# A two-layer hybrid decoder on one core: block sums of the feed-forward activations formed in its first part, three feature pairs summed in PSUM in the second, mLSTM scores on full rows

## The chip, the cores and the metric

The kernel runs on 1 core of one Trainium2 chip, as one program. The metric is the time of one execution on the device, in microseconds, as the median of several runs. Its engines are TensorE (PE: matmuls; PEld: weight loads beside them), VectorE (DVE), ScalarE (ACT), GpSimd (POOL) and SyncE (SP), whose queue issues the DMA transfers.

## The reference

Two layers, sequence 1024, width 1024, all in float32. A layer has four token mixers side by side, an output projection, a LayerNorm, a gated feed-forward block and a second LayerNorm. The change touches the mLSTM mixer and the feed-forward block:

```python
def _mlstm_chunkwise(q, k, v, i_pre, f_pre):          # chunks of 128, 4 heads of 64
    ...
        d_log = b_cum[:, :, :, None] - b_cum[:, :, None, :] + ic[:, :, None, :]
        d_log = jnp.where(causal, d_log, -jnp.inf)
        ...
        w_intra = jnp.exp(d_log - m_t[..., None])
        sqk = jnp.einsum('bthd,bshd->bhts', qc, kc) * w_intra
        ...
h = (jax.nn.silu(x @ w_gate[l]) * (x @ w_up[l])) @ w_down[l]     # 1024 -> 2816 -> 1024
x = _layer_norm(DEEPNORM_ALPHA * x + h, ln2_g[l], ln2_b[l])
```

## The kernel before

**Precision.** The large products are float32 to some 22 bits: each operand is split into a high half in the matmul type fp32r (ScalarE casts) and a low half (the difference, on VectorE or GpSimd), and three matmuls of 128x512 make one product: high-high, high-low, low-high. Each tile of 1024 columns holds both halves of 512.

**Order of the work.** The Tile framework places the instructions: within each engine they stand in an order that it chooses by program order and by a simulated timeline, with waits for data and for free buffers. Only in the mLSTM (`mix_d`) is PE's order that of the program. SP issues DMAs in its queue's order.

**mLSTM (`mix_d`).** Eight chunks of 128 tokens. Per chunk, `stage_s` forms a row of weights (`pw`: a matmul that selects one row of `NC`, 40 rows high), four exponentials on ScalarE, a causal mask on GpSimd, and the scores `psc`: for each of 4 heads a float32 matmul of 64 rows by 128 columns (TensorE runs it as two passes), the heads of odd number on rows 64 to 127, each followed by two of the next chunk's projection matmuls (`zvo`, `self.fill(2)`). VectorE multiplies scores and weights in two operations. `stage_n` and `stage_u` make the output and the state update (`pi`, `pn`, `pk`, `pu`, updates of `ds`); `stage_y` transposes the output (`ptd`). All of these have full 128 rows. `stage_s(c + 1)` runs ahead of `stage_n(c)`.

**First part of the feed-forward (`ffn1`, `evac1`).** The hidden features are taken as 11 pairs of 128-feature tiles, the tokens as two halves of 512. Each 2x2 block product is made with 7 products (Strassen's scheme in Winograd's form, numbers 1 to 7 in the order `ORDER = (1, 6, 2, 7, 5, 3, 4)`) instead of 8. A gate tile m and the up tile m + 1 follow each other; `evac1` adds the products up on VectorE into `Ra`, `Rb` (pool R, 8 buffers), applies SiLU to the gate and multiplies. The four blocks of a pair go to `hs` in DRAM as two tiles of 512 KB. The weights `fw` come through 4 buffers, are combined and split into `fc` (6 buffers), four products ahead.

**Second part (`ffn2`).** The same 7-product scheme over 9 pairs; the last two pairs (`std`) go by plain products (`dl`). For each pair `load` brings two tiles of h (`hr`) and two of w (`dr`), `combos` forms the sums of their blocks (four VectorE operations for h, four for w) and splits them: the high half on ScalarE, the low half on GpSimd, for w of the pairs 1, 3 and 5 on VectorE. The pairs are taken in groups: pair 0 alone, then two and two. A step is one group and one product number. In a step each of the four row blocks j opens one PSUM bank, sums 3 matmuls per pair of the group there (`dn`), and closes it; then VectorE adds the bank to an accumulator in SBUF (`ma`, `mb`, `mc`, `md`; in the first group ScalarE copies into ma and mb). mc and md start as x1, the input of the block. In the last group `finish` joins the accumulators, one to three VectorE operations per step and j. `comb` prepares operands up to `AHEAD = 2` steps before their use, in 14 tiles (`operand`). Eight PSUM banks rotate. Behind the groups, `hsplit` and two loops split h and w of the last two pairs, and `dl` products, the second LayerNorm and, in layer 1, the transposes (`ptx`) for the next layer follow.

Of the kernel before, what the change touches and what calls it, by code (L numbers as in the profile page):

```python
# [7 lines left out]
F32 = mybir.dt.float32  # L8
# [5 lines left out]
L = 2  # L14
# [43 lines left out]
class Net:  # L58
# [85 lines left out]
    def consts(self):  # L144
# [5 lines left out]
        sel = cp.tile([40, 8], F32, name="self32")  # L150
        nc.sync.dma_start(sel, io["c_sel"])
        self.sel = cp.tile([40, 8], F32R, name="sel")
# [229 lines left out]
    def mix_d(self, l, T):  # L382
# [6 lines left out]
        def gates():  # L389
# [75 lines left out]
            NC = dr[0:40, 0:512]  # L465
            nc.vector.tensor_scalar(out=NC, in0=self.ident[0:40, 0:1].to_broadcast([40, 512]), scalar1=0.0, scalar2=None, op0=ALU.mult)
# [117 lines left out]

        def stage_s(c):
            tok = tok_of(c)
            pw = self.psum("pw", "mm")
            nc.tensor.matmul(pw, lhsT=self.sel[:, c:c + 1].to_broadcast([40, 128]), rhs=NC, start=True, stop=True)
# [11 lines left out]
            for e_ in range(2):  # L600
                w2 = w4[:, e_:4:2, :]
                nc.vector.tensor_tensor(out=w2, in0=psc[e_][:, 0:256].rearrange("p (h t) -> p h t", h=2), in1=w2, op=ALU.mult)
# [74 lines left out]
        nc.vector.memset(Cf, 0.0)  # L677
        stage_s(0)
# [682 lines left out]
    def evac1(self, l, m, i, pz, R):  # L1361
# [44 lines left out]
        if up and i == (5 if early else 3):  # L1406
            nc.sync.dma_start(io["hs"][l, 2 * f], ra)
        if up and i == 4:
            nc.sync.dma_start(io["hs"][l, 2 * f + 1], rb)
            R.pop(m - 1), R.pop(m)  # L1410

    def ffn2(self, l, last):
# [4 lines left out]
        self.open(x=4, b=4, a=4, c=4, d=4, p=6, o=4)  # L1417
        raws, cmb = {}, {}

        def load(q):  # L1420
            hr = [self.u("hr", F32, "A") for _ in range(2)]
            wr = [self.u("dr", F32, "A") for _ in range(2)]
            for i in range(2):
                nc.sync.dma_start(wr[i], io["wD"][l, 2 * q + i])
                nc.sync.dma_start(hr[i], io["hs"][l, 2 * q + i])
            raws[q] = (hr, wr)
# [6 lines left out]
        groups = [[0]] + [[q, q + 1] for q in range(1, NP - 2, 2)]  # L1433
        std = [NP - 2, NP - 1]

        steps = [(g, i) for g in range(len(groups)) for i in ((1, 6, 7, 5) if g == 0 else ORDER)]
# [4 lines left out]
        def operand(s):  # L1441
            nonlocal nx
            nx += 1
            return self.u(s, F32R, "ooooppppppxxxx"[(nx - 1) % 14])

        def comb(g, i):
            for q in (groups[0] if g == 1 and i in early else []) + groups[g]:
                if q not in cmb:
                    if q not in raws:
                        load(q)  # L1450
                    (h0, h1), (w0, w1) = raws[q]
                    s2 = [self.t2("s2") if g == 0 else None for _ in range(2)]
                    cmb[q] = (self.combos("S", h0[:, lo_], h1[:, lo_], h0[:, hi_], h1[:, hi_], self.t2("s1"), nc.gpsimd, v, s2[0]),
                              self.combos("T", w0[:, lo_], w0[:, hi_], w1[:, lo_], w1[:, hi_], self.t2("s1"), v if q in (1, 3, 5) else nc.gpsimd, v, s2[1]))
                ts = []
                for x in range(2):
                    t = operand("dc")
                    cmb[q][x][i](t)
                    ts.append(t)
                Wc.setdefault((g, i), []).append(ts)  # L1460
# [224 lines left out]
```

## Time and profile before

| | us |
|---|---|
| median of 3 runs (2536.72 to 2543.18) | 2540.49 |
| the profiled execution | 2537.39 |
| its span, first to last instruction | 2535.7 |
| PE busy in it | 2405.2 (95%) |
| DVE busy | 1674.2 (66%) |
| POOL busy | 1347.0 (53%) |
| ACT busy | 1038.7 (41%) |

A line of the timeline gives the start, the time from the first start to the last end of the merged instructions, the engine, the line of the kernel, the operation with output and inputs, their number, and in brackets how long the engine had been idle and who released it. Matmuls overlap: one of 128x512 shows as some 0.39 us, but the next starts 0.23 us after it, so their pitch is read from starts. The clock column is the granted TensorE clock, 1.00 for 2.4 GHz and 0.50 for 1.2 GHz; a mean between stands for a stretch that had both.

### The profile page before, as it was taken

To read this page: it belongs to the slowest core of one execution; us is meant where nothing else is said; L and a number is where in the kernel's file an instruction comes from. 1 tells how busy PE (TensorE), PEld (TensorE's weight loads), DVE (VectorE), ACT (ScalarE), POOL (GpSimd) and SP (SyncE) were. 2 spreads that over 40 slices of the span, in tenths; PEclk is the share of its full clock that TensorE was granted. 3 is DMA by queue.
4 is the path that set the end of the run, shared out by engine and by line. 5 is a ranking of instruction groups with operands and counts; after the bars stand their busy time and mean duration, and the time that the engine had idled before them with its cause. 6 is when DMAs were issued, how large, how long until landed. Compare 5 with 4: busy or idle time off the path is not lost. (4 is left out here: it accounts for less than half of the span.)

```text
span 2535.7 us, 33381 instructions
## 1 busy us (share of the span) xinstructions
PE 2405.2 (95%) x11884; PEld 1993.6 (79%) x11884; DVE 1674.2 (66%) x3040; ACT 1038.7 (41%) x2102; POOL 1347.0 (53%) x1148
## 2 busy tenths in 40 slices
PE   9999878998999999999899999889989999999997
PEld 9779867786888888777697798777868888887775
DVE  7643587478545555999956435874785455559998
ACT  6323568534332333434243235685343323334431
POOL 2013546667554444889520145366665454557894
PEclk9999999999999999999999999899999999999998
DMA  4101101421222224512221110014212222245221
GB/s 162 51 27 41 29 9 56 158 100 54 79 83 95 72 84 150 199 74 76 79 89 43 33 40 23 9 56 158 100 66 69 88 94 67 84 157 192 75 75 67
DMA packets 62807, 206.95 MB, mean 82 GB/s; under 512 B 8546, under 2 KB 10914, under 8 KB 62642
## 3 DMA queue, kind: packets, MB, share of 16 engines
q1 hardware_dynamic: 62642, 204.82, 23.3%
q8 instruction: 95, 1.56, 0.2%
q14 instruction: 70, 0.57, 0.1%
HBM read 158.62 MB, written 46.17 MB: 81 GB/s over the span
## 5 line engine op out<-in xcount | busy, mean ns | idle before, releaser
L119 PE MATMUL gu<-T,fc 128*128 128x512 f32 x2640 | 636.1, 397 | 18.7 <-POOL T L1323 6.1
L119 PEld LDWEIGHTS gu<-T,fc 128*128 128x128 f32 x2640 | 499.6, 190 | 141.6 <-POOL T L1323 8.4
L1248 POOL TENSOR_TENSOR fc<-fw,fc 128x512 fp32r<-128x512 f32 x264 | 366.9, 1393 | 366.5 <-ACT fc L1247 362.5
L119 PE MATMUL dn<-dc,dc 128*128 128x512 f32 x1512 | 361.6, 399 | 20.0 <-DVE md L1512 5.4
L119 PEld LDWEIGHTS dn<-dc,dc 128*128 128x128 f32 x1512 | 285.3, 190 | 96.0 <-DVE ma L1512 7.8
L1247 ACT CAST fc<-fw 128x512 fp32r<-128x512 f32 x264 | 162.7, 620 | 379.3 <-PE gu L119 212.0
L1372 DVE TENSOR_TENSOR Ra<-Ra,gu 128x512 f32<-128x512 f32 x172 | 117.4, 684 | 228.8 <-PE gu L119 225.7
L119 PE MATMUL gu<-B,fc 128*128 128x512 f32 x1056 | 260.5, 395 | 0.0
L119 PEld LDWEIGHTS gu<-B,fc 128*128 128x128 f32 x1056 | 197.8, 188 | 46.9
L1248 POOL TENSOR_TENSOR dc<-hr,dc 128x512 fp32r<-128x512 f32 x104 | 167.8, 1622 | 46.4 <-ACT dc L1247 45.6
L805 POOL TENSOR_SCALAR P<-P,rs 128x256 f32<-128x256 f32 (+7 forms) x128 | 99.5, 782 | 126.7 <-DVE rs L804 108.4
L119 PE MATMUL po<-wh,yT 128*128 128x512 f32 x512 | 162.2, 396 | 0.0
L132 POOL TENSOR_TENSOR wl<-raw,wh 128x768 fp32r<-128x768 f32 (+2 forms) x40 | 81.9, 2054 | 114.8 <-ACT wh L127 114.6
L119 PE MATMUL zc<-wh,xT 128*128 128x384 f32 x512 | 134.1, 339 | 0.0
L1247 ACT CAST dc<-hr 128x512 fp32r<-128x512 f32 x104 | 64.6, 621 | 150.7 <-PE dn L119 47.0
L119 PE MATMUL sc<-kst,q 128*128 128x512 f32 (+3 forms) x384 | 110.9, 384 | 13.6 <-DVE mn L798 13.5
L822 PE MATMUL pt<-ident,P 128*128 128x128 f32 x576 | 92.1, 283 | 23.3 <-DVE PL L141 14.4
L119 PEld LDWEIGHTS po<-wh,yT 128*128 128x128 f32 x512 | 95.7, 188 | 21.8
L802 ACT ACTIVATE P<-P,mn 128x256 f32<-128x256 f32 (+7 forms) x128 | 99.5, 779 | 27.0 <-DVE mn L798 25.4
L1248 POOL TENSOR_TENSOR dc<-dr,dc 128x512 fp32r<-128x512 f32 x68 | 109.1, 1605 | 0.0
L119 PE MATMUL dl<-wl,hl 128*128 128x512 f32 x384 | 97.5, 412 | 11.7 <-DVE mc L1512 9.6
L141 DVE TENSOR_TENSOR PL<-pt,PH 128x512 fp32r<-128x512 f32 (+3 forms) x176 | 95.0, 558 | 20.5 <-ACT PH L138 19.4
(380 smaller groups left out, 5123.9 us busy)
## 6 DMA issues: line engine op xcount, KB each, us to landing
fw<-in_wGU SPq DMA_DIRECT2D x88, 512.0 KB, 3.7
dr<-in_wD SPq DMA_DIRECT2D x44, 512.0 KB, 5.8
hr<-hs SPq DMA_DIRECT2D x44, 512.0 KB, 6.2
hs<-Ra SPq DMA_DIRECT2D x22, 512.0 KB, 2.6
hs<-Rb SPq DMA_DIRECT2D x22, 512.0 KB, 2.9
raw<-in_wO SPq DMA_DIRECT2D x16, 512.0 KB, 3.6
x<-x SPq DMA_DIRECT2D x16, 512.0 KB, 2.6
raw<-in_wC SPq DMA_DIRECT2D x16, 384.0 KB, 3.0
```

The costliest lines, as they stand in the source:

```text
L119: self.nc.tensor.matmul(out, lhsT=a, rhs=b, start=first and j == 0, stop=last and j == n - 1)
L132: (eng or nc.gpsimd).tensor_sub(lo[:, :n], raw[:, :n], f32(hi[:, :n]))
L141: (lo_eng or nc.vector).tensor_sub(lo, src, f32(hi))
L802: nc.scalar.activation(P[:, 0:nk], P[:, 0:nk], AF.Exp, scale=-1.0, bias=m, accum_out=rs[:, 0:1])
L805: nc.gpsimd.tensor_scalar(out=P[:, 0:nk], in0=P[:, 0:nk], scalar1=rs[:, 1:2], scalar2=1.0, op0=ALU.mult, op1=ALU.mult)
L822: nc.tensor.transpose(pt[:, b * 128:(b + 1) * 128], P[:, (b0 + b) * 128:(b0 + b + 1) * 128], self.ident)
L1247: nc.scalar.copy(dst[:, 0:512], src)
L1248: lo_eng.tensor_sub(dst[:, 512:1024], src, f32(dst[:, 0:512]))
L1372: tt = lambda o, a, b, op: v.tensor_tensor(out=o, in0=a, in1=b, op=op)
```

## The change

Three things.

1. mLSTM: the selecting matmul `pw` reads 128 rows of `NC` (the others are zero). The queries of a chunk are copied by GpSimd (`spread`, four copies of 64x128) into a zeroed tile `qz`, two heads side by side as diagonal blocks, two chunks ahead. The scores are then two matmuls of 128 rows by 256 columns into one bank, each followed by four `zvo` matmuls, and one VectorE multiplication.
2. ffn1: for the 9 pairs that take the 7-product scheme in ffn2, `evac1` forms the block sums of h (four more VectorE operations, in the gate's freed tiles) and stores all in `hs` as four parts, 1.75 MB a pair instead of 1 MB.
3. ffn2: three groups of three pairs. `comb` loads each half tile of h (256 KB, pool h of 6 half tiles) that a step needs, split by ScalarE and GpSimd; only w is combined, its low halves on GpSimd for one pair of three and on VectorE for two. A step opens four banks and takes one pair after the other, 12 matmuls each; the banks close at the end. 15 operand tiles; `AHEAD = 1`. w of the next group is loaded in the third step of a group, x1 at the first and fourth step.

```diff
+    def uh(self, s, dt=F32, p="h"):
+        return self.pools[p].tile([128, 512], dt, name=self.nm(s), tag="h" + p)
...
-            NC = dr[0:40, 0:512]
+            NC = dr[:, 0:512]
...
+        qz = self.u("qz", F32, "E")
+        nc.gpsimd.memset(qz, 0.0)
+        QZ = [[qz[:, (2 * b + p) * 256:(2 * b + p + 1) * 256] for p in range(2)] for b in range(2)]
...
-            nc.tensor.matmul(pw, lhsT=self.sel[:, c:c + 1].to_broadcast([40, 128]), rhs=NC, start=True, stop=True)
+            nc.tensor.matmul(pw, lhsT=self.sel[:, c:c + 1].to_broadcast([128, 128]), rhs=NC, start=True, stop=True)
...
-            psc = [self.psum("psc", "s") for _ in range(2)]
-            for hh in range(4):
-                rows = slice(64 * (hh % 2), 64 * (hh % 2) + 64)
-                nc.tensor.matmul(psc[hh % 2][:, hh // 2 * 128:(hh // 2 + 1) * 128], lhsT=QK[2 + hh // 2][rows, tok], rhs=QK[hh // 2][rows, tok], start=True, stop=True)
-                self.fill(2)
...
+            psc = self.psum("psc", "s")
+            for pr_ in range(2):
+                nc.tensor.matmul(psc[:, pr_ * 256:(pr_ + 1) * 256], lhsT=QK[2 + pr_][:, tok], rhs=QZ[c % 2][pr_], start=True, stop=True)
+                self.fill(4)
+            nc.vector.tensor_tensor(out=w, in0=psc, in1=w, op=ALU.mult)
+            spread(c + 2)
...
+        def spread(c):
+            if c < NT:
+                for p in range(2):
+                    for e in range(2):
+                        rows = slice(64 * e, 64 * e + 64)
+                        nc.gpsimd.tensor_copy(QZ[c % 2][p][rows, e * 128:(e + 1) * 128], QK[p][rows, tok_of(c)])
...
-        if up and i == (5 if early else 3):
-            nc.sync.dma_start(io["hs"][l, 2 * f], ra)
...
+        st = f < NP - 2
+        if i == (5 if early else 3):
+            if st:
+                tt(ga[:, 0:512], r[0], r[1], sub)
+                tt(r[1], r[1], r[3], add)
+                tt(ga[:, 512:1024], r[1], r[0], sub)
+                nc.sync.dma_start(io["hs"][l, f, 2], ga)
+            nc.sync.dma_start(io["hs"][l, f, 0], ra)
+        if i == 4:
+            nc.sync.dma_start(io["hs"][l, f, 1], rb)
+            if st:
+                tt(gb_[:, 0:512], r[2], ga[:, 512:1024], sub)
+                nc.sync.dma_start(io["hs"][l, f, 3][:, 0:512], gb_[:, 0:512])
...
-        self.open(x=4, b=4, a=4, c=4, d=4, p=6, o=4)
+        self.open(x=4, b=4, a=4, c=4, d=4, p=6, o=1, h=6)
...
-        groups = [[0]] + [[q, q + 1] for q in range(1, NP - 2, 2)]
+        groups = [[0, 1, 2], [3, 4, 5], [6, 7, 8]]
...
+                    cmb[q] = self.combos("T", w0[:, lo_], w0[:, hi_], w1[:, lo_], w1[:, hi_], self.t2("s1"), nc.gpsimd if n == 2 else v, v)
+                p, cs = part[i]
+                hr = self.uh("hr")
+                nc.sync.dma_start(hr, io["hs"][l, q, p][:, cs])
+                H, W = operand("dc"), operand("dc")
+                self.split(H[:, lo_], H[:, hi_], hr, lo_eng=nc.gpsimd)
+                cmb[q][i](W)
...
-            return self.u(s, F32R, "ooooppppppxxxx"[(nx - 1) % 14])
+            return self.u(s, F32R, "ppppppoxxxxAAAA"[(nx - 1) % 15])
...
-        AHEAD = 2
+        AHEAD = 1
...
-            if i == 6 and g + 1 < len(groups):
-                for q in groups[g + 1]:
+            if n % 7 == 2:
+                for q in groups[g + 1] if g + 1 < len(groups) else std:
                     load(q)
-            if g == 0 and i == 7:
+            if n == 0:
                 for j in range(4):
                     c.append(self.u("mc", F32, "c"))
                     nc.sync.dma_start(c[j], io["x1"][l, j * 128:(j + 1) * 128, :])
+            if n == 3:
                 for j in range(4):
                     d.append(self.u("md", F32, "d"))
...
+            pz = [self.bank("dn") for _ in range(4)]
+            for x, (H, Wt) in enumerate(ops):
+                wh, wl = Wt[:, lo_], Wt[:, hi_]
+                for j in range(4):
+                    hh, hl = H[:, j * 128:j * 128 + 128], H[:, 512 + j * 128:640 + j * 128]
+                    self.mms(pz[j], [(hh, wh), (hh, wl), (hl, wh)], first=x == 0, last=x + 1 == len(ops))
...
         def hsplit(h):
             for q in std:
                 for i in range(2):
+                    hr = self.uh("hr")
+                    nc.sync.dma_start(hr, io["hs"][l, q, i][:, h * 512:(h + 1) * 512])
                     t = operand("hl")
```

## Rows read from the trace of the kernel before

**Rows 1.** the page: busy time of each engine (us, share of the span, instructions).
```profile
PE 2405.2 (95%) x11884; PEld 1993.6 (79%) x11884; DVE 1674.2 (66%) x3040; ACT 1038.7 (41%) x2102; POOL 1347.0 (53%) x1148
```

**Rows 2.** timeline of PE in ffn2: start, us, line, count, idle before.
```profile
2277.65 4.82 PE L119 MATMUL dn<-dc,dc 128*128 128x512 f32 x20
2397.58 70.59 PE L119 MATMUL dn<-dc,dc 128*128 128x512 f32 x306 [2.14 <-DVE md L1512]
2468.05 0.47 PE L119 MATMUL dl<-wl,hl 128*128 128x512 f32 x1
2475.37 46.32 PE L119 MATMUL dl<-wl,hl 128*128 128x512 f32 x188 [4.80 <-DVE mc L1512]
...
1209.54 26.72 PE L119 MATMUL dl<-wl,hl 128*128 128x512 f32 x104 [4.78 <-DVE mc L1512]
```

**Rows 3.** windows of ffn2: length, each engine's busy us (count), PE clock, DMA share, GB/s.
```profile
2278.00:2301.00 23.00, 18.42 (x76) 13.62 (x74) 22.93 (x23) 17.21 (x34) 18.75 (x12) 0.98 0.88 330
2430.00:2468.00 38.00, 38.00 (x167) 30.86 (x165) 36.81 (x44) 14.41 (x25) 38.00 (x24) 1.00 0.05 14
2468.00:2490.00 22.00, 16.11 (x57) 12.46 (x57) 20.29 (x26) 1.65 (x3) 3.63 (x3) 0.84 0.00 1
```

**Rows 4.** waits of PE in 1010 to 1270: us in total, times, longest.
```profile
PE dn L119 <- DVE ma L1512: 2.2, 3, 1.2
```

**Rows 5.** groups of DVE and POOL in layer 1's dn: busy us, mean ns.
```profile
L1248 DVE TENSOR_TENSOR dc<-dr,dc 128x512 fp32r<-128x512 f32 x18 | 21.8, 1212 | 0.0
L1512 DVE TENSOR_TENSOR ma<-ma,dn 128x512 f32<-128x512 f32 x32 | 20.9, 677 | 3.6 <-PE dn L119 3.6
...
L1248 POOL TENSOR_TENSOR dc<-hr,dc 128x512 fp32r<-128x512 f32 x51 | 82.8, 1632 | 21.6 <-ACT dc L1247 20.9 <-DMA dr<-in_wD 0.6
```

**Rows 6.** timelines of POOL beside VectorE, and of VectorE with POOL idle.
```profile
1017.62 3.45 POOL L1248 TENSOR_TENSOR dc<-s,dc 128x512 fp32r<-128x512 f32 x2
...
1219.42 2.48 DVE L1461 TENSOR_TENSOR mb<-mb,md 128x512 f32<-128x512 f32 x4
```

**Rows 7.** ffn1 in steady state: window of all engines, timelines of SP, POOL, PE.
```profile
760.00:800.00 40.00, 40.00 (x174) 32.39 (x173) 20.02 (x26) 12.25 (x21) 19.28 (x15) 1.00 0.24 79
...
780.12 0.33 SPq L1409 DMA_DIRECT2D hs<-Rb  x1
...
786.68 1.28 POOL L1248 TENSOR_TENSOR fc<-fw,fc 128x512 fp32r<-128x512 f32 x1 [1.51 <-ACT fc L1247]
...
796.85 2.95 PE L119 MATMUL gu<-B,fc 128*128 128x512 f32 x12
```

**Rows 8.** one steady mLSTM chunk: window of all engines, timelines of POOL and DVE.
```profile
142.30:152.80 10.50, 10.50 (x54) 7.71 (x53) 4.51 (x14) 1.91 (x8) 0.77 (x2) 1.00 0.01 2
...
144.18 0.63 POOL L594 TENSOR_SCALAR_AFFINE_SELECT w<-w 128x512 f32<-128x512 f32 x1 [9.78 <-ACT w L592]
...
141.99 0.90 DVE L624 SCALAR_TENSOR_TENSOR ds<-ds,pu 64x66 f32<-64x66 f32 x3
```

**Rows 9.** timeline of PE in a steady mLSTM chunk.
```profile
139.34 0.38 PE L609 MATMUL pk<-ident,qk 128*128 128x128 f32 x2
139.47 0.48 PE L564 MATMUL zvo<-wl,xT 128*128 128x512 f32 x1
...
141.95 0.38 PE L668 MATMUL ptd<-ident,df 128*128 128x128 f32 x2
142.26 0.50 PE L588 MATMUL pw<-dr,sel 40*128 40x512 f32 x1
...
146.69 0.39 PE L636 MATMUL pi<-ds,qk 128*128 128x132 f32 x2
```

**Rows 10.** timeline of PE in the first chunk's scores.
```profile
109.50 0.93 PE L598 MATMUL psc<-qk,qk 64*128 64x128 f32 x8
110.36 0.49 PE L564 MATMUL zvo<-wh,xT 128*128 128x512 f32 x1
```

**Rows 11.** DMA issues in layer 1's ffn2: count, KB, median us to landing.
```profile
hr<-hs SPq DMA_DIRECT2D x15, 512.0 KB, 6.3
```

More of the change, by code (lines that the diff above doesn't have):

```diff
@@ L149, in consts @@
         nc.vector.tensor_copy(self.identr, self.ident)
-        sel = cp.tile([40, 8], F32, name="self32")
+        sel = cp.tile([128, 8], F32, name="self32")
         nc.sync.dma_start(sel, io["c_sel"])
-        self.sel = cp.tile([40, 8], F32R, name="sel")
+        self.sel = cp.tile([128, 8], F32R, name="sel")
         nc.vector.tensor_copy(self.sel, sel)
@@ L1405, in evac1 @@
                 tt(r[q], r[q], g, ALU.mult)
-        if up and i == (5 if early else 3):
-            nc.sync.dma_start(io["hs"][l, 2 * f], ra)
-        if up and i == 4:
-            nc.sync.dma_start(io["hs"][l, 2 * f + 1], rb)
+        if not up:
+            return
+        ga, gb_ = R[m - 1]
+        st = f < NP - 2
[11 more added lines that the diff above has]
+                nc.sync.dma_start(io["hs"][l, f, 3][:, 0:512], gb_[:, 0:512])
             R.pop(m - 1), R.pop(m)
@@ L1416, in ffn2 @@
         self.close()
[L1417 removed]
+        self.open(x=4, b=4, a=4, c=4, d=4, p=6, o=1, h=6)
         raws, cmb = {}, {}
         def load(q):
[L1421 to L1422 removed]
+            raws[q] = [self.u("dr", F32, "A") for _ in range(2)]
             for i in range(2):
[L1424 to L1426 removed]
+                nc.sync.dma_start(raws[q][i], io["wD"][l, 2 * q + i])
         a, b, c, d = [], [], [], []
@@ L1432, in ffn2 @@
         slot = {1: (a, lo_), 6: (a, hi_), 7: (b, lo_), 5: (b, hi_), 2: (c, lo_), 3: (c, hi_), 4: (d, lo_)}
-        groups = [[0]] + [[q, q + 1] for q in range(1, NP - 2, 2)]
+        part = {1: (0, lo_), 5: (0, hi_), 2: (1, lo_), 4: (1, hi_), 7: (2, lo_), 6: (2, hi_), 3: (3, lo_)}
+        groups = [[0, 1, 2], [3, 4, 5], [6, 7, 8]]
         std = [NP - 2, NP - 1]
-        steps = [(g, i) for g in range(len(groups)) for i in ((1, 6, 7, 5) if g == 0 else ORDER)]
+        steps = [(g, i) for g in range(len(groups)) for i in ((1, 6, 7, 5, 2, 3, 4) if g == 0 else ORDER)]
         early = (2, 3, 4)
@@ L1443, in operand @@
             nx += 1
-            return self.u(s, F32R, "ooooppppppxxxx"[(nx - 1) % 14])
+            return self.u(s, F32R, "ppppppoxxxxAAAA"[(nx - 1) % 15])
         def comb(g, i):
-            for q in (groups[0] if g == 1 and i in early else []) + groups[g]:
+            for n, q in enumerate(groups[g]):
                 if q not in cmb:
@@ L1450, in comb @@
                         load(q)
[L1451 to L1460, printed above, removed]
+                    w0, w1 = raws[q]
+                    cmb[q] = self.combos("T", w0[:, lo_], w0[:, hi_], w1[:, lo_], w1[:, hi_], self.t2("s1"), nc.gpsimd if n == 2 else v, v)
[5 more added lines that the diff above has]
+                cmb[q][i](W)
+                Wc.setdefault((g, i), []).append((H, W))
         tt = lambda eng, o, x, y, op: eng.tensor_tensor(out=o, in0=x, in1=y, op=op)
@@ L1485, in ffn2 @@
                 done += 1
-            if i == 6 and g + 1 < len(groups):
-                for q in groups[g + 1]:
+            if n % 7 == 2:
+                for q in groups[g + 1] if g + 1 < len(groups) else std:
                     load(q)
-            if i == 6 and g + 1 == len(groups):
-                for q in std:
-                    load(q)
-            if g == 0 and i == 7:
+            if n == 0:
                 for j in range(4):
@@ L1643, in layouts @@
     o["c_ident"] = np.eye(128, dtype=np.float32)
-    sel = np.zeros((40, 8), np.float32)
+    sel = np.zeros((128, 8), np.float32)
     sel[np.arange(8), np.arange(8)] = 1.0
@@ L1677 @@
     io["x1"] = nc.dram_tensor("x1", (L, S, D), F32, kind="Internal").ap()
-    io["hs"] = nc.dram_tensor("hs", (L, NF, 128, S), F32, kind="Internal").ap()
+    io["hs"] = nc.dram_tensor("hs", (L, NP, 4, 128, S), F32, kind="Internal").ap()
     io["xs"] = nc.dram_tensor("xs", (S, D), F32, kind="Internal").ap()
```

27 lines of the change are left out of this document (9 added, 18 removed).

## The prediction, made before the changed kernel ran

> **What bounds the kernel now.** I read the page first: TensorE is busy for 95% of the span [rows 1]. With such a page a change can win in two ways only: TensorE work goes away, or the places where TensorE waits or runs at half clock go away. So I next held each stage against the pure pitch of its matmuls. The pitch comes from the longest unbroken run: 306 matmuls of 128x512 from 2397.58 to 2468.05, 0.230 us each [rows 2].
>
> Second feed-forward part (ffn2): 756 dn and 192 dl matmuls a layer, 948 x 0.230 = 218 us. In layer 2 it runs from 2277.65 to 2475.37 + 46.32 = 2521.7, 244 us: 26 too many [rows 2]. They split into dn (190.4 us for 174 of work: 16), the seam, where four dl matmuls take 7.3 us instead of 0.9 (6.4), and the other 188 dl (46.3 us for 43.3: 3, at a granted clock of 0.84 in the window behind the seam [rows 3]). Layer 1 has the same wait at its seam, 4.78 us ahead of 1209.54 [rows 2]; I take it as alike. The list of waits names VectorE's evictions for dn too, 2.2 us for ma alone [rows 4]. VectorE is busy for 36.8 of 38 us before the seam, POOL for all 38 [rows 3].
>
> Why is VectorE late? Its evictions from PSUM take 0.68 us, its subtractions with both inputs in SBUF 1.21, POOL's 1.63 [rows 5]. Where both have such work they go in step, one operation each every 1.7 us (two of POOL's take 3.45); VectorE with POOL idle does four in 2.48, one every 0.60 [rows 6], and POOL alone takes 1.28 [rows 7]. So in ffn2 POOL and VectorE together are the second bound, close behind TensorE.
>
> mLSTM stage: TensorE has no gap; VectorE is busy for 4.5 of 10.5 us, ACT 1.9, POOL 0.8 [rows 8]. A chunk costs what its matmuls cost.
>
> **The change part by part.**
> *mLSTM without row modes.* In a steady chunk the score stage goes from pw at 142.26 to pi at 146.69, 4.43 us [rows 9], and holds pw, four score products of K=64 and eight zvo fills. At the pitch the fills are 8 x 0.23 = 1.84 and pw 0.23. The scores with little switching: the first chunk has all eight passes (two to a float32 product) back to back, from 109.50 to 110.36, 0.86 us [rows 10]. Sum 2.93, so 1.5 of the 4.43 us goes to changing between 40, 64 and 128 rows. After the change there are two products of K=128 with 256 columns: the same 1024 pass columns, 0.86 us. Besides, ptd to pw takes 0.31 where pk to the next product takes 0.13: about 0.17 of the same kind [rows 9]. Seven chunks a layer have the interleaved form, five of them behind a ptd: 7 x 1.5 + 5 x 0.17 = 11.3 us, 22.6 in two layers (bounds 18 and 25: a wider product might cost up to 0.3 a chunk more, or the first chunk's 0.86 still hold some switching). The first chunk gains nothing. What is added: four POOL copies of 64x128 a chunk, each between nothing and the 0.63 us of the 512-column select, 2.5 at most, where POOL is idle for 9.7 of 10.5 us [rows 8]; a copy is for the chunk after the next. Were that cover gone, 2.5 us a chunk would eat the gain. On POOL the copies stand ahead of the next chunk's select, which has a whole chunk to spare. One VectorE product of 512 columns replaces two of 256: nothing. The zeroing of NC keeps its 512 columns. The state chain ends at 142.89 and pi needs it at 146.69 [rows 8, 9]: 3.8 us to spare, 2.2 afterwards. The zero tile takes one more buffer of E; the last chunk's scores free it before the next stage fills E. Nothing.
>
> *First part (ffn1).* Nine feature pairs a layer get four more VectorE operations each, 0.6 to 1.7 us apiece. In steady state VectorE is busy for 20 of 40 us and TensorE for all 40 [rows 7]: hidden, since eight PSUM banks hold 8 x 2.8 us of products and an eviction may come 3 us late. Each pair also stores 768 KB more. SP issues in order, and weight loads stand behind the store at 780.12; behind it now comes one more store, which waits for one more subtraction, 0.6 to 1.8 us. The next split from a weight tile that I can place is at 786.68, and its product is the one at 796.85, so some 8 us are spare [rows 7]. Cost 0; without that cover 1.8 x 18 = 32 us.
>
> *Second part (ffn2).* The products stay 756 + 192. VectorE's operations in a layer: combinations 72 to 36 (those of h have moved), low halves of w 21 to 42 (two pairs of three, formerly q = 1, 3, 5), evictions 112 to 68 (21 steps of four for 32, 16 by ACT in both), the joining 32. Sum 237 to 178; with both inputs in SBUF 125 to 110. POOL's low halves 105 to 84. ACT keeps 126 casts.
> Groups 0 and 1: three pairs are 252 matmuls, 58 us. POOL has 28 operations, at 1.7 in step 48 us; VectorE's 26 SBUF operations fit beside them, and its 12 to 28 evictions between. A group of two pairs gave TensorE 38.7 us, and POOL 21 to 28 operations, 36 to 48 us. So the waits in the middle should go: 0 to 4 us stay, I take 1.
> Start: the first step needs three pairs (3 MB of w, 0.75 of h) where one sufficed, but one after the other, each for 12 matmuls, 2.8 us. An h load lands in 6.3 us [rows 11]. Four 512 KB loads of x1 now stand on SP ahead of the h loads of the third step. Bounds 0 and 7 us; the first 23 us now hold 76 matmuls (17.5 us), a loss of 5.5 [rows 3]. I take 3, since pair by pair hides part of what now shows.
> End: the last group has 12 + 14 + 32 = 58 SBUF operations and 28 evictions on VectorE, 28 on POOL, then the splits of std's w and h. 28 x 1.7 = 48, 30 x 0.60 = 18, some 9 for std: 75 us, less about 6 done ahead, against 58: VectorE ends 11 us late. The same count today is 48 + 20 x 0.60 + 9 = 69 against 38.7, less 10 done ahead: 20 late, and in layer 1 the joining indeed goes on until 1221.9, 12 us after the wait at the seam [rows 2, 6] and 20 after dn. The dl products take the banks of the last two steps, so 11 us of lateness costs some 4 (0 to 7), and the clock behind it 2 to 3. I take 7 where it is 9 now.
> Left: 3 + 1 + 7 = 11 of 26 us, a gain of 15 a layer, 30 in all (bounds 3 and 26 a layer). Buffers: a step takes six operand tiles of 15 and gives two back every 2.8 us; an h tile has two steps, 16 us, for 6.3 of landing and 2 to 3 of cast and split. Hidden.
> The Trainium skill, "SBUF — State Buffer", section "Who interferes with whom", says that a VectorE instruction with two SBUF inputs and a GpSimd instruction that reads SBUF exclude each other for the whole instruction, which speaks against handing VectorE 21 more such subtractions. By that rule a pair would cost 0.60 + 1.28 = 1.88 us, an estimate; the last group would end 16 us late and not 11, and the time would be some 10 us higher, inside the range. The trace agrees that they block, though its 1.7 us a pair leave some overlap.
>
> **Sum.** The profiled execution took 2537.4 us (span 2535.7, and 1.7 around it): 2537.4 - 22.6 - 30 = 2484.8. The median of the runs is 3.1 above it, so 2488.
>
> **The rivals.**
> 1. *VectorE and POOL stay late in ffn2.* The start loses 8 us as loads queue behind x1, the last group 15 as joining and splitting go in step with POOL. For it: both engines are full before the seam [rows 3]. Against: 59 fewer VectorE operations. ffn2 then gives 3 a layer: 2537.4 - 22.6 - 6 + 3.1 = 2512. Chance 0.20.
> 2. *mLSTM doesn't do what the change says*: with fewer switches the chunk is held by another thing (the copies, the state chain, a dearer wide product). Against it: nothing but TensorE is over half busy there [rows 8]. 22.6 comes back: 2511. Chance 0.07; together with the first, 2534, 0.04.
> 3. *Slower: a step starves.* The look-ahead goes from two steps to one, and h comes step by step through six small tiles. If an h load is issued only when the step before begins to compute, each step waits 6.3 + 1.6 = 8 us for its first pair, with the other two pairs' 5.6 as cover: 2.4 us x 42 steps = 100 us, so 2588. It decides from a wait of 53 / 42 = 1.3 us a step. Against it: the tiles hold two steps. Chance 0.07.
> 4. *All of ffn2's loss comes back*: 52 + 22.6: 2466. Chance 0.07.
>
> **How the numbers follow.** Forecast 0.55, rivals as above. The range takes in the forecast's bounds and rivals 1, 2 and 4, 2466 to 2516, and leaves out the starving step and the double miss. A measurement of this kernel tells 0.3% (7.6 us) from no change. Faster, below 2533: 0.55 + 0.20 + 0.07 + 0.07 = 0.89; within it the double miss, 0.04; slower 0.07.
>
> **What would show it.** mLSTM: score stage 2.9 us, no gap put down to "issue" ahead of psc, a chunk of 8.9. ffn1: as long as now, no wait for fw. ffn2: dn 178 us, no waits for evictions in the middle, a wait for mc or md at the seam of 7 at most. It is wrong if TensorE waits for dc from ACT or POOL (operands late), if the landing of hr leads the waits, or if the clock falls inside the middle groups.

## The result and the profile after

The changed kernel takes 2477.86 us (median of 4 runs, 2474.35 to 2480.23) where the kernel before takes 2541.31 beside it: a ratio of 0.9752, interval 0.9734 to 0.977. It is 2.5% faster; 2488 was forecast, with 2466 to 2516 around it. The profiled execution took 2477.19 us with a span of 2475.5, 60.2 less than before.

Where the 60.2 us were is read from the timeline of PE alone, from the first matmul of each stage to the first of the next, in us. Layer 2's mLSTM lies between the last `zdq` and the last `zb`:

| stage | before | after | difference | in the forecast |
|---|---|---|---|---|
| start to first gu of layer 1 (mLSTM in it) | 565.6 | 554.6 | -11.0 | -11.3 |
| ffn1, layers 1 and 2 | 445.8, 445.7 | 446.5, 446.9 | +1.9 | 0 |
| dn, layers 1 and 2 | 190.9, 190.6 | 179.8, 179.6 | -22.2 | -24 |
| dl, layers 1 and 2 | 57.5, 53.6 | 52.9, 48.7 | -9.4 | -6 |
| last dl to last zdq (layer 2's first projections) | 109.4 | 104.3 | -5.1 | 0 |
| last zdq to last zb (mLSTM of layer 2) | 113.7 | 102.6 | -11.1 | -11.3 |
| last zb to first gu of layer 2 | 348.9 | 348.9 | 0 | 0 |
| last dl to the end | 14.0 | 10.8 | -3.2 | 0 |

Below, "the seam to layer 2" or "the layer seam" is the stretch from the last dl product of layer 1 to the last `zdq`, and the tail is the one behind the last dl product of layer 2.

The same places of the profile after. The page's line of busy times; VectorE and POOL do less, as counted, against [rows 1]:

```profile
PE 2373.0 (96%) x11820; PEld 1992.1 (80%) x11820; DVE 1662.9 (67%) x2978; ACT 1040.0 (42%) x2102; POOL 1308.8 (53%) x1172
```

A steady mLSTM chunk, timeline of PE and, for the copies, of POOL (start, us, engine, line; answers [rows 8, 9]):

```profile
127.74 0.38 PE L683 MATMUL ptd<-ident,df 128*128 128x128 f32 x2
127.88 0.47 PE L605 MATMUL pw<-dr,sel 128*128 128x512 f32 x1
128.19 0.59 PE L614 MATMUL psc<-qz,qk 128*128 128x256 f32 x2
...
128.85 0.63 POOL L600 COPY qz<-qk 64x128 f32<-64x128 f32 x2 [6.03 <-PE psc L614]
...
130.91 0.39 PE L651 MATMUL pi<-ds,qk 128*128 128x132 f32 x2
...
136.72 0.38 PE L683 MATMUL ptd<-ident,df 128*128 128x128 f32 x2
```

From pw to pi 3.03 us (4.43 before, 2.93 forecast), from ptd to pw 0.14 (0.31 before), the chunk 8.98 (8.9 forecast). Two copies take 0.63 together, and nobody waits for them.

ffn2, timeline of PE, layer 1 and then layer 2 (answers [rows 2]); in brackets the idle time before and who ended it:

```profile
1001.14 1.09 PE L123 MATMUL dn<-dc,dc 128*128 128x512 f32 x4
1004.65 176.43 PE L123 MATMUL dn<-dc,dc 128*128 128x512 f32 x752 [2.42 <-DVE dc L1265]
1180.91 4.79 PE L123 MATMUL dl<-wl,hl 128*128 128x512 f32 x20
...
2236.46 1.09 PE L123 MATMUL dn<-dc,dc 128*128 128x512 f32 x4
2239.99 176.19 PE L123 MATMUL dn<-dc,dc 128*128 128x512 f32 x752 [2.44 <-DVE dc L1265]
2416.02 4.81 PE L123 MATMUL dl<-wl,hl 128*128 128x512 f32 x20
2422.90 41.77 PE L123 MATMUL dl<-wl,hl 128*128 128x512 f32 x172 [2.07 <-DVE wl L145]
```

One wait of 2.4 us is left in dn, four matmuls after its start, and one of 2.1 in dl; the waits for evictions [rows 4] are gone. Windows of the same stage (as [rows 3]):

```profile
2236.00:2246.00 10.00, 7.56 (x26) 5.81 (x25) 8.37 (x10) 4.98 (x9) 7.16 (x6) 0.83 0.88 278
2296.00:2356.00 60.00, 60.00 (x260) 48.60 (x259) 53.59 (x57) 24.60 (x45) 46.69 (x31) 1.00 0.45 152
2416.00:2428.00 12.00, 9.93 (x36) 7.62 (x35) 12.00 (x15) 1.14 (x2) 3.59 (x2) 0.86 0.00 0
```

In the middle TensorE is busy throughout at full clock, and neither VectorE (53.6 of 60) nor POOL (46.7) is full. Both ends lose: the granted clock is 0.83 at the start and 0.86 behind dn, where VectorE is busy for all 12 us. The groups of layer 1's dn (as [rows 5]), the last of VectorE's joining, and the landing of h (as [rows 11]):

```profile
L1265 DVE TENSOR_TENSOR dc<-dr,dc 128x512 fp32r<-128x512 f32 x36 | 45.7, 1280 | 17.4 <-ACT dc L1264 17.4
L1535 DVE TENSOR_TENSOR ma<-ma,dn 128x512 f32<-128x512 f32 x16 | 10.3, 676 | 1.8 <-PE dn L123 1.8
...
L145 POOL TENSOR_TENSOR dc<-hr,dc 128x512 fp32r<-128x512 f32 x61 | 93.9, 1554 | 33.7 <-ACT dc L142 30.4 <-PE dn L123 3.3
...
2425.16 2.48 DVE L1488 TENSOR_TENSOR mb<-mb,md 128x512 f32<-128x512 f32 x4
...
hr<-hs SPq DMA_DIRECT2D x64, 256.0 KB, 2.8
```

VectorE ends the joining at 2427.6, 11.6 us behind the last dn product; before it was 2487.7 against 2468.05, 19.7.

The head of the seam to layer 2, timeline of PE, before and then after:

```profile
1261.80 0.63 PE L1127 MATMUL ptx<-ident,mb 128*128 128x128 f32 x4 [2.10 <-DVE xT L141]
1263.77 0.80 PE L119 MATMUL za<-wh,xT 128*128 128x264 f32 x2 [1.34 <-ACT wh L127]
...
1233.65 0.60 PE L1144 MATMUL ptx<-ident,mb 128*128 128x128 f32 x4
```

Before, TensorE waits here 2.1 us for VectorE's `xT` and 1.3 for ScalarE's operand of `za`, and the granted clock is 0.66 over the first 10 us of this seam. After, it goes on without a wait there, and the clock is 1.00.

### The profile page after: what moved, and what is told of

It is laid out like the page before. It is cut to its first block, busy times and chain, and to the rows that moved or that the text cites. A ratio compares the mean times of both kernels' runs of the same rounds, so it can differ in the third digit from the quotient of the medians.

```text
span 2475.5 us, 33577 instructions
## 1 busy us (share of the span) xinstructions
PE 2373.0 (96%) x11820; PEld 1992.1 (80%) x11820; DVE 1662.9 (67%) x2978; ACT 1040.0 (42%) x2102; POOL 1308.8 (53%) x1172
## 4 chain that ended last, share of the span: by engine, by line
PE 76%; DVE 11%; ACT 5%; POOL 4%; issue 3%; DMA 1%; POOLq 0%; DVEq 0%; ACTq 0%; SPq 0%
PE gu L123 33%; PE dn L123 13%; PE zc L123 5%; PE po L123 4%; PE zvo L568 4%; PE zdq L520 3%; PE za L123 3%; PE zb L123 2%; PE sc L123 2%; PE pv L860 2%; DVE P L815 1%; PE pt L839 1%; ACT P L819 1%; DVE PL L145 1%; POOL x L1132 1%
## 5 line engine op out<-in xcount | busy, mean ns | idle before, releaser
L1265 POOL TENSOR_TENSOR fc<-fw,fc 128x512 fp32r<-128x512 f32 x264 | 374.2, 1421 | 362.4 <-ACT fc L1264 358.1
L123 PE MATMUL dn<-dc,dc 128*128 128x512 f32 x1512 | 354.8, 397 | 4.9 <-DVE dc L1265 4.9
L145 POOL TENSOR_TENSOR dc<-hr,dc 128x512 fp32r<-128x512 f32 x126 | 195.0, 1562 | 87.6 <-ACT dc L142 80.8
L123 PE MATMUL sc<-kst,q 128*128 128x512 f32 (+3 forms) x384 | 111.5, 387 | 12.5 <-DVE mn L815 12.5
L1265 DVE TENSOR_TENSOR dc<-dr,dc 128x512 fp32r<-128x512 f32 x72 | 90.2, 1264 | 32.9 <-ACT dc L1264 32.8
L142 ACT CAST dc<-hr 128x512 fp32r<-128x512 f32 x126 | 77.7, 622 | 82.1 <-DMA hr<-hs 53.8
L123 PE MATMUL po<-wl,yT 128*128 128x512 f32 x256 | 100.2, 394 | 0.0
```

The source lines that it names most:

```text
L123: self.nc.tensor.matmul(out, lhsT=a, rhs=b, start=first and j == 0, stop=last and j == n - 1)
L142: nc.scalar.copy(hi, src)
L145: (lo_eng or nc.vector).tensor_sub(lo, src, f32(hi))
L1265: lo_eng.tensor_sub(dst[:, 512:1024], src, f32(dst[:, 0:512]))
```

## The experiments

Theory: the mLSTM gains what its changes between row modes cost, and ffn2 gains because less work of VectorE and POOL makes VectorE less late behind dn. Against it stand: that full rows as such are cheaper; that the sums over three pairs in four open banks matter, not the move of the block sums; that VectorE's lateness is hidden. The kernels were run in four sets, and the kernel before, measured beside each, took 2536.5 to 2541.9 us; so small differences between sets are read from the ratios. For every run the table gives its median and, from the profiled run's timeline of PE in layer 2, the length of dn, how late VectorE ended the joining behind dn, and the length of dl (192 products at 0.230 us are 44.2); in the run with two pairs on POOL the wait ahead of the first dl product is counted to dl.

| kernel | us | ratio to before | dn | late | dl |
|---|---|---|---|---|---|
| before | 2541.3 | 1 | 190.6 | 19.7 | 53.6 |
| mLSTM's part alone | 2521.1 | 0.9915 [0.99, 0.9929] | 194.5 | 18.6 | 51.7 |
| before, scores in a row | 2514.3 | 0.9893 [0.9878, 0.9907] | 190.5 | 19.7 | 52.6 |
| before, block sums moved alone | 2515.6 | 0.9895 [0.9878, 0.9911] | 178.8 | 17.2 | 49.7 |
| after | 2477.9 | 0.9752 [0.9734, 0.977] | 179.6 | 11.6 | 48.7 |
| after, bank by bank | 2484.7 | 0.9771 [0.9755, 0.9786] | 177.6 | 14.7 | 53.6 |
| after, joining left out | 2466.5 | 0.9718 [0.9693, 0.9744] | 178.1 | | 44.7 |
| after, scores in a row | 2475.7 | 0.9758 [0.9735, 0.9781] | 178.0 | 11.6 | 47.1 |
| after, first pair's low halves on POOL | 2480.2 | 0.9775 [0.9752, 0.9797] | 180.4 | 9.9 | 45.3 |
| after, two pairs' low halves on POOL | 2490.5 | 0.9814 [0.9791, 0.9836] | 178.2 | 17.6 | 53.4 |
| after, two steps ahead | 2471.0 | 0.9732 [0.9715, 0.975] | 178.9 | 10.1 | 45.4 |
| after, wl on POOL | 2474.9 | 0.9754 [0.9736, 0.9771] | 178.2 | 11.9 | 48.5 |
| after, wl and one join on POOL | 2473.6 | 0.9744 [0.9726, 0.9762] | 178.0 | 9.1 | 44.7 |
| four edits together | 2473.3 | 0.9745 [0.9724, 0.9765] | 178.5 | 10.5 | 45.7 |

### The mLSTM

**Its part alone, in the kernel before** (sel, NC, qz, spread and the two wide products as in the change).

> The kernel before with the mLSTM part of the change alone (scores and selecting matmul on 128 rows). If the gain there is the time of switching between row modes and stays to the end: about 22 us under the kernel before, 2518, a chunk 9.0 us instead of 10.56, the rest of the timeline moved as a whole. If the faster chunk is given back later (attention, output projection), less than 10 us, 2530 or more.

2521.12 us, 20.7 less than before. Layer 2's mLSTM took 102.5 us (113.7 before, 102.6 after), the first gu came at 556.9 (565.6). This part does what the changed kernel shows, without the rest.

**The row modes kept, only the order of the four scores changed.**

```diff
                 nc.tensor.matmul(psc[hh % 2][...], lhsT=QK[2 + hh // 2][rows, tok], ...)
-                self.fill(2)
+            self.fill(8)
```

> The kernel before; only the order of one chunk's matmuls is changed: the four score products of 64 rows follow each other and the eight projection matmuls come behind them. If each entry into and exit from a row mode costs time, three of four entries go, about 1.1 us in 14 chunks, 15 us: 2525. If it is the half-filled product itself that is slow, nothing moves: 2540.

2514.28 us: as good as full rows, which neither side expected. The chunk in its timeline of PE:

```profile
128.24 0.38 PE L668 MATMUL ptd<-ident,df 128*128 128x128 f32 x2
128.55 0.50 PE L588 MATMUL pw<-dr,sel 40*128 40x512 f32 x1
128.56 0.94 PE L598 MATMUL psc<-qk,qk 64*128 64x128 f32 x8
129.43 0.50 PE L564 MATMUL zvo<-wh,xT 128*128 128x512 f32 x1
...
131.40 0.39 PE L636 MATMUL pi<-ds,qk 128*128 128x132 f32 x2
```

From pw to pi 2.85 us. ptd to pw is 0.31, as before: a change of mode stands there. The 0.17 lost there and the 0.18 gained after it cancel, and layer 2's mLSTM took 102.3 us. So the 4.43 us of before paid for coming back to the fills three times more: 1.58 us, 0.53 a time. The Trainium skill ("TensorEngine Tiling (Array Packing)", section "Tiling Modes") says that a change of mode, not one of the tile, drains TensorE; the trace agrees, since the eight passes change tiles and pay nothing. The 6.8 us between this run and the one before it lie outside the mLSTM: the largest piece is the stretch from the last zb to gu (350.6 against 346.3), which neither edit touches (dn differs by 4 us in layer 2 and by 3.3 the other way in layer 1). Their mean granted clocks are 0.976 and 0.98, and by the clock records of the two traces work at half clock costs 52.5 us in one and 45.3 in the other, which is the whole difference of the spans.

**The same in the changed kernel** (no qz, no copies on POOL, 40 and 64 rows).

> The changed kernel with the mLSTM of the kernel before, 64-row scores and 40-row pw kept, the four score products of a chunk in a row and the eight fill products behind them (no zero-padded copies on POOL). In the run of that edit alone on the kernel before, the chunk took 8.97 us, against 8.98 in the changed kernel and some 10.4 before, but the time was 6.6 us under the kernel with full rows alone. Theory: the price was the number of switches between row modes, not the row modes, and the 6.6 us lie outside the mLSTM (granted clock, dn of layer 2 and the seam): 2474 to 2481, the same as the changed kernel. Rival: row modes in a row are truly cheaper than full rows by the padded copies that POOL no longer makes: 2468 to 2473.

2475.66 us, within the changed kernel's 2474.35 to 2480.23; mLSTM of layer 2 102.4 us. Full rows, the zero tile and the copies were not needed: the gain is the number of switches.

### Which part of ffn2's change

**The block sums moved to ffn1, groups [0], [1, 2], ... and the banks as before.**

```diff
+            if st:
+                tt(ga[:, 0:512], r[0], r[1], sub)
...
-                    cmb[q] = (self.combos("S", h0[:, lo_], ...), self.combos("T", w0[:, lo_], ...))
+                    cmb[q] = self.combos("T", w0[:, lo_], ..., v if q in (1, 3, 5) else nc.gpsimd, v, s2)
```

> The kernel before with the block sums of h formed in the first part, groups of two pairs and one bank after the other as before. If VectorE and GpSimd together bound the second part, 36 operations fewer a layer with both inputs in SBUF give 8 to 12 us a layer: about 2520. If what counts is the number of evictions and GpSimd's 105 splits, which stay, less than 6 us in all: 2535 or more.

2515.64 us, 26.2 less: the theory, by more than expected. Timeline of PE in layer 2's ffn2, then the end of VectorE's joining:

```profile
2269.97 3.67 PE L123 MATMUL dn<-dc,dc 128*128 128x512 f32 x8 [3.22 <-ACT dc L1251]
2274.62 174.32 PE L123 MATMUL dn<-dc,dc 128*128 128x512 f32 x748 [0.98 <-POOL dc L1252]
2448.77 1.87 PE L123 MATMUL dl<-wl,hl 128*128 128x512 f32 x7
2453.66 2.85 PE L123 MATMUL dl<-wl,hl 128*128 128x512 f32 x7 [3.02 <-DVE mc L1527]
...
2464.08 1.89 DVE L1476 TENSOR_TENSOR mb<-mb,md 128x512 f32<-128x512 f32 x3
```

748 matmuls without a gap: all that dn could win is won by the move, with pairs two and two. What three pairs and four open banks add lies elsewhere: VectorE 11.6 us late instead of 17.2, dl 1.1 to 1.8 us shorter a layer, the tail 10.8 for 15.7, the seam to layer 2 104.3 for 107.7, ffn1 446.9 for 451.2 in layer 2 (3.2 of it the wait ahead of the first dn product in the lines above). Run alone, the mLSTM's part and this one give 20.7 and 26.2 of the 63.5 us; the other 16 belong to the rest of the ffn2 change and to the parts' meeting. Groups of three without the other edits were not run.

**The changed kernel with one bank after the other** (j outside, the three pairs inside).

```diff
-            for x, (H, Wt) in enumerate(ops):
-                for j in range(4):
+            for j in range(4):
+                pz[j] = self.bank("dn")
+                for x, (H, Wt) in enumerate(ops):
```

> The changed kernel; within a step the banks are filled one after the other, each over all three pairs, in place of four open banks with pair after pair. If pair by pair is what lets a step start with one pair's operands, each layer loses 3 to 8 us at its start and where operands come late: 2484 to 2494. If operands are always a step ahead, nothing: 2478 within 3.

2484.71 us, 6.9 more than the change (4.8 by the ratios, whose intervals overlap), inside what the theory gave, but by another road: dn is even shorter (177.6), and the loss is at the end, where TensorE waits twice for wl:

```profile
2422.68 0.97 PE L123 MATMUL dl<-wl,hl 128*128 128x512 f32 x3 [3.20 <-DVE wl L145]
2426.60 46.12 PE L123 MATMUL dl<-wl,hl 128*128 128x512 f32 x188 [2.96 <-DVE wl L145]
```

So, as far as this profile shows, four open banks serve through the order of VectorE's work behind dn, not through the start of a step, where I had seen their use.

### Is VectorE's lateness what counts?

**The joining left out.**

```diff
                 if g + 1 == len(groups):
-                    finish(i, j)
+                    pass
```

> The changed kernel with the joining left out: the 28 VectorE additions a layer that combine the seven product blocks into the four quarters of the output in the third group's steps are not issued, so the output is not the reference's; everything else stands as in the changed kernel. Measured so far: with the change the 172 ffn2 products end, and VectorE is still busy with the joining for 11.6 us; TensorE then waits 2.1 us for VectorE's low halves of wl. Theory: what the change gave in the dl stage, at the layer seam and in the tail (4.6 + 4.9, about 5, 3.2 us, none of it in the sum of the prediction at that size) came because VectorE enters the dl stage less late; so taking its remaining work away gives more at just those places: both dl stages shorter by 2 to 4 us each, the layer seam and the tail by 1 to 4 together, no wait of dl for wl: 2464 to 2471. Rival: the dl stage is bounded by its own 212 products at .230 us and the layer norm chain behind them, and VectorE's lateness there is hidden: 2475 to 2479, and the seam and the tail are of another origin.

2466.49 us, 11.4 less (8.6 by the ratios, whose intervals just overlap), as the theory had it. The edit leaves out all of `finish`, 32 VectorE operations a layer (28 and four that also scale). Timeline of PE in layer 2:

```profile
2236.29 174.73 PE L123 MATMUL dn<-dc,dc 128*128 128x512 f32 x752 [2.47 <-DVE dc L1265]
2410.86 44.69 PE L123 MATMUL dl<-wl,hl 128*128 128x512 f32 x192
```

dl runs at the pitch, 44.7 us instead of 48.7, and in layer 1 49.0 instead of 52.9; the tail is 9.4 instead of 10.8. The seam to layer 2 stays at 104.5, but for two reasons that cancel: TensorE idles there for 3.1 us and not 4.2, and half clock behind a wait in its middle, which the profile of the change was spared, costs 1.7 (more on this where the prediction is gone through).

**Operands two steps ahead, as in the kernel before.**

```diff
-        AHEAD = 1
+        AHEAD = 2
```

> The changed kernel with operands of ffn2 prepared two steps ahead as in the kernel before, not one; all else as in the change. Theory: VectorE and POOL have fixed work in ffn2 and are the late ones at its ends, and operands made earlier in a ring of 15 tiles free nothing: 2475 to 2481. At the start two steps' six operand pairs stand ahead of the first evictions on VectorE and ACT; the PSUM banks wait for them there: if so up to 5 us a layer slower, 2480 to 2488. Rival: the start wait of 2.4 us and the low clock behind it come from too little lead, and go: 2468 to 2474.

2470.98 us, 6.9 less than the change (5 by the ratios, whose intervals overlap). The time is the rival's, the mechanism is not: the wait at the start stays, 2.42 us, and the gain is at the end.

```profile
2237.55 66.15 PE L123 MATMUL dn<-dc,dc 128*128 128x512 f32 x284 [2.42 <-DVE dc L1265]
2304.34 108.72 PE L123 MATMUL dn<-dc,dc 128*128 128x512 f32 x468 [0.64 <-DVE md L1537]
2412.90 4.82 PE L123 MATMUL dl<-wl,hl 128*128 128x512 f32 x20
2418.23 40.11 PE L123 MATMUL dl<-wl,hl 128*128 128x512 f32 x172 [0.51 <-DVE wl L145]
```

VectorE is 10.1 us late, the wait for wl is 0.5 and not 2.1, and dl takes 45.4; one wait of 0.64 in the middle is new. No work has left the end: VectorE's operations behind dn are the same, and in the 180 us ahead of it VectorE is busy for 159.8 us where it was 158.9. What differs is who goes first there. VectorE's additions and POOL's splits, in the change and then here:

```profile
2417.62 4.09 DVE L1488 TENSOR_TENSOR ma<-ma,mc 128x512 f32<-128x512 f32 x3
2416.97 3.59 POOL L145 TENSOR_TENSOR hl<-hr,hl 128x512 fp32r<-128x512 f32 x2 [1.55 <-ACT hl L142]
...
2415.16 1.88 DVE L1488 TENSOR_TENSOR ma<-ma,mc 128x512 f32<-128x512 f32 x3
2413.84 6.76 POOL L145 TENSOR_TENSOR hl<-hr,hl 128x512 fp32r<-128x512 f32 x2 [1.50 <-ACT hl L142]
```

In the change the two engines go in step; here VectorE's three additions run at their pitch alone, and POOL's two splits take 6.76 us. The run with the first pair's low halves on POOL, below, has the same order (1.89 and 6.54 us) and dl 45.3 with a look-ahead of one. So the gain in dl is that of an order at the end of dn; that looking further ahead brings it about is not shown. Part of it goes back: the tail takes 12.5 us for 10.8.

### Work given to POOL

**Two pairs' low halves of w on POOL**, one pair in the change.

```diff
-..., nc.gpsimd if n == 2 else v, v)
+..., nc.gpsimd if n >= 1 else v, v)
```

> The changed kernel with the low halves of two of the three pairs' weight sums in every group made on POOL (one of three in the change): 21 splits a layer leave VectorE, some 0.7 to 1.2 us each, and come to POOL at 1.3 to 1.75 us each. In the changed kernel's middle stretches VectorE was busy 54 of 58 us and POOL 39 to 44 of 58. Theory: VectorE is the engine that ends late, POOL has about 55 us free a layer and takes 21 x 1.6 = 34 of them, VectorE ends the joining earlier by up to 7 of the third group's splits, 5 to 8 us, which shows in the dl stages: 2468 to 2474. Rival: POOL becomes the late one, and its longer holds make VectorE's additions longer too (in the kernel before a split beside POOL's work took 1.2 us and not .69): TensorE waits for POOL's low halves: 2480 to 2500.

2490.46 us, 12.6 more (15.8 by the ratios). TensorE does not wait for POOL, as the rival had it, but for VectorE, which ends later though it has less to do. Groups of layer 1's dn, and PE in layer 2:

```profile
L1265 POOL TENSOR_TENSOR dc<-dr,dc 128x512 fp32r<-128x512 f32 x36 | 55.4, 1547 | 0.0
...
L1265 DVE TENSOR_TENSOR dc<-dr,dc 128x512 fp32r<-128x512 f32 x18 | 32.8, 1823 | 20.1 <-ACT dc L1264 20.0
...
2430.37 46.87 PE L123 MATMUL dl<-wl,hl 128*128 128x512 f32 x192 [6.51 <-DVE mc L1535]
```

VectorE's remaining 18 take 1.82 us each and not 1.28: half of the operations saves 45.7 - 32.8 = 12.9 us, not 22.8, and POOL's lasts 1.55. In layer 1's two middle windows of 60 us POOL is busy for 55 and 53, in one of layer 2 for all 60. VectorE is 17.6 us late. Longer operations are not all of that: in the last 59 us of layer 2's dn VectorE is busy for 49.1 only (55.5 in the change) and waits 8.5 us for ScalarE's casts (1.2 in the change). The Trainium skill ("SBUF — State Buffer", section "Who interferes with whom") has it that two such instructions exclude each other; the 1.82 is near its sum of the two alone, 0.60 + 1.28 = 1.88, an estimate, so here, with POOL at work for nine tenths of the time, the trace agrees with the rule.

**The first pair's low halves on POOL**, for the wait at the start.

```diff
-..., nc.gpsimd if n == 2 else v, v)
+..., nc.gpsimd if n == 2 or q == 0 else v, v)
```

> The changed kernel with the low halves of the first pair's weight sums (7 of them a layer) made on POOL and not on VectorE. At the start of ffn2 TensorE waits 2.4 us for the first of these, which VectorE made 1.77 us long at 1002.82, behind ffn1's last block sums. Theory: that wait is VectorE's order at the seam; on POOL, idle there until 997.7, the low half is ready before the first product ends, the wait of 2.4 us goes in both layers and the stretch at granted clock .81 behind it may go too, and VectorE ends 7 x .7 us less late in nothing, since these are the first group's: 2470 to 2475. Rival: POOL has the three splits of H to make there, 1.3 to 1.5 us each, so the low half is late on POOL in turn, TensorE waits for POOL: 2477 to 2483.

2480.16 us, the rival's time: the same as the change, by the ratios' intervals. The wait of 2.4 is gone, and VectorE is 9.9 late by the order at the end described above; other waits came, in layer 2:

```profile
2243.19 6.01 PE L123 MATMUL dn<-dc,dc 128*128 128x512 f32 x24 [0.92 <-POOL dc L1265]
2249.49 60.78 PE L123 MATMUL dn<-dc,dc 128*128 128x512 f32 x260 [0.29 <-ACT dc L1264]
2310.65 1.64 PE L123 MATMUL dn<-dc,dc 128*128 128x512 f32 x6 [0.38 <-DVE md L1537]
2313.50 108.22 PE L123 MATMUL dn<-dc,dc 128*128 128x512 f32 x462 [1.22 <-DVE md L1537]
```

**The last two low halves of wl on POOL**, which is idle there.

```diff
-                self.split(hi, lo, w)
+                self.split(hi, lo, w, lo_eng=nc.gpsimd if q == std[1] else None)
```

> The changed kernel with the low halves of the last two of the dl stage's four weight tiles (wl) made on POOL, which the profile of the changed kernel shows idle for 8.35 us at that place, and not on VectorE, which makes them at 2416.48 and 2421.64 between the joining's additions while TensorE waits 2.1 us for the second. Theory: in the dl stage every microsecond that leaves VectorE between the end of dn and the end of the joining is one of the span; two splits of 1.14 us a layer and the wait go, POOL's two (some 2.6 us each) are done before dn ends: 2 to 4 us a layer, 2470 to 2475. Rival: POOL's splits of 1024 columns make VectorE's additions beside them longer (.69 to 1.8 us was seen) or delay the hl splits behind them on POOL, and nothing is gained: 2476 to 2480, or more.

2474.94 us, at the edge of what the theory gave and within the changed kernel's own range. The profile is on the rival's side: dl is 48.5 us, VectorE as late as ever (11.9). POOL's two take 6.02 us beside VectorE's joining, and the wait has only moved, from wl to a bank:

```profile
2408.48 6.02 POOL L145 TENSOR_TENSOR wl<-dr,wl 128x1024 fp32r<-128x1024 f32 x2 [5.03 <-PE dn L123]
...
2421.43 40.79 PE L123 MATMUL dl<-wl,hl 128*128 128x512 f32 x168 [1.98 <-DVE md L1535]
```

**That, and one of the joining's blocks on POOL too.**

```diff
-                tt(v, A1, A1, c[j][:, hi_], add)
+                tt(nc.gpsimd, A1, A1, c[j][:, hi_], add)
```

> As the run with wl's low halves on POOL, and the four additions that join the block of the last step but one (ma<-ma,mc; 4.1 us of VectorE's path after dn's end) on POOL too. Theory, VectorE's work behind dn alone counts: a further 2 to 4 us a layer, 2465 to 2470. Rival: the four take POOL some 6 us, and VectorE's first addition to dl's product waits for them, or they hold up the two beside them: no further gain or a loss, 2473 to 2482.

2473.58 us (2469.45 to 2476.65). dl of layer 2 runs at the pitch, 44.7 us in one piece, as with no joining at all, and VectorE is 9.1 late; and dl of layer 1 49.0. Yet of these 8 us only 3.6 reached the span: the first gu came 2.5 us later (557.1), the seam to layer 2 took 107.8 for 104.3 and the tail 12.3 for 10.8. The time is the rival's.

**Together**: scores in a row, two steps ahead, wl and one join on POOL.

> The changed kernel with four edits together: the mLSTM of the kernel before with its four score products in a row, operands of ffn2 two steps ahead, the last two low halves of wl on POOL, and the additions that join the last step but one's block on POOL. Alone they gave 2475.7, 2471.0, 2474.9 and (the last two together) 2473.6, where the changed kernel took 2477.9 and that without the joining 2466.5. Theory: two steps ahead and the work given to POOL take the same few microseconds, VectorE's lateness behind dn, whose dl stage was at 44.7 to 45.4 us in layer 2 with either and at 44.7 without the joining; so together they give little beyond the better one: 2467 to 2472. Rival: they add, each from its own part: 2460 to 2466. Or they collide on POOL, which then has operands and joining at once: over 2473.

2473.34 us (2471.45 to 2478.61): they don't add, and on POOL they collide a little. dl is 45.7 us in layer 2, where two steps ahead alone has 45.4; TensorE now waits 0.78 for POOL's wl. Its profile is of the slowest of the five runs (2478.61 us): 4 us more went between the last zb and gu (353.2 for 348.9), where nothing was edited. So the complete kernel with the best median is the change with `AHEAD = 2`, 2470.98 us, 0.9732 [0.9715, 0.975]; its interval overlaps those of the change, of these four edits and of the runs with wl on POOL, so that it is the faster one is not shown.

## Why the prediction came out as it did

- **mLSTM, -22.6 forecast:** -22.1. The sum over switches was right in every part (3.03 for 2.93 us, 0.14 for 0.13, the copies hidden). What I didn't see is that the same arithmetic also prices an order with fewer switches and no full rows; the runs with the scores in a row show that this is worth as much.
- **ffn1, 0 forecast:** +1.9 in two layers. The cover holds.
- **ffn2, -30 forecast:** -31.6. Of the 26 us lost in layer 2, 10 are left (11 forecast): start 5.6 for 3 (2.4 of wait, the rest low clock and a slow first step), middle 0 for 1, end 4.5 for 7. The joining's lateness was 11.6 for 11. Its price was a mis-sized term: 11.6 us late cost 4.5 in dl, not 7 (2.1 of wait, most of the rest half clock behind it), and 9.1 to 10.1 us cost 0.5 to 1.2, by the three kernels with dl at 44.7 to 45.4. Lateness alone doesn't set the price either: bank by bank 14.7 us went with dl at 53.6, and with the block sums moved alone 17.2 went with 49.7. And the reason given for the middle, that fewer evictions and longer groups let POOL and VectorE through, is not needed: moving the sums of h clears the middle by itself.
- **Nothing forecast behind ffn2:** -8.3, of which 5.1 at the seam to layer 2 and 3.2 in the tail. This is the step that failed: the sum ended with the last dl product, as if nothing behind it hung on the change. By the traces and their clock records, 2.5 of the 5.1 us are a loss to half clock that is gone and 1.4 are waits that are gone; the rest is not resolved. A part is luck: in the middle of this seam the change and all nine of its variants have a wait of about 3 us for `ds`. In the variants the granted clock then falls to half for a few microseconds (0.83 over 10 us with two steps ahead), in the profile of the change it stays 1.00. So the seam is 104.3 in the change and 104.5 to 107.9 in the variants, against 107.7 to 109.4 with groups of two pairs. The tail is 14.0 in the kernels before the ffn2 change, 15.7 with only the sums moved and 9.4 to 12.5 in the kernels made from the change; that its length hangs on when VectorE, POOL and ACT reach the last two tiles is read from the chain of waits, not shown by a run of its own. It takes back some of what dl gains: 12.3 to 12.5 us in the four kernels with dl at 44.7 to 45.7 and the joining in it, 10.8 with dl at 48.7.
- **The median:** 10 below the forecast: 7.6 from the span (60.2 - 52.6), and 2.4 since the profiled run of before lay 3.1 below its median and that of after 0.7.
- **The rivals:** the first (VectorE and POOL stay late) has its mechanism in the run with two pairs on POOL, not in the change. The starving step did not come: 256 KB of h land in 2.8 us (median). ScalarE's casts wait for hr five times in layer 1, 15.5 us in all; TensorE has no wait from it. That all of ffn2's loss comes back would have taken 20 us more.

## What to carry to other kernels

When a second engine ends a stage late, count its work in that stage's last group, and look at what a third engine does beside it there: the same three additions took 4.09 us in step with POOL and 1.88 ahead of it, and with that went 3 us of the next stage. Follow the gain to the end, too: here the stages behind took part of it back. Moving work to an engine that shares the memory path isn't free, even where that engine idles: 18 subtractions fewer saved VectorE 13 us of 23 in layer 1, and the kernel got slower by 12.6. Where a matrix engine changes row modes, put what shares a mode in a row before widening it with zeros.

## What the runs showed of the hardware

- Going into a 64-row mode and back cost 0.53 us a time between products of 128 rows, with no gap in the busy time of PE but in its pitch; eight passes of 64 rows in a row took 0.87 us; with full rows 0.96 is left for the same columns (3.03 less nine products at 0.23).
- VectorE's operations of 128x512 with both inputs in SBUF: one every 0.60 us alone; its subtractions 1.21 to 1.28 in the mean with POOL partly at work, 1.82 with POOL at work for nine tenths of the time. Where both have work, either can come first: three VectorE additions and two POOL splits at one place took 4.09 and 3.59 us in one kernel, 1.88 and 6.76 in another.
- A stretch that no edit touched (last zb to gu, layer 2) took 346.2 to 353.2 us in the profiled runs, and dn of the old form 190.5 to 194.5: a single profile's stage is good to some 4 us, and effects under that, of which several above are, are as uncertain as that. In the first of these two stages TensorE is idle for 27 to 30 us in all of them, and its mean granted clock is 0.98 in the shortest and 0.96 in the longest.
